# A whole decoder trunk ordered by the scheduler's other model machine

## The chip, the cores and the metric

One Trainium2 chip, one of its cores. The metric is the device time of one execution in microseconds (us): the median of several runs of the kernel before is 1920.45 us (three runs, 1916.95 to 1922.32). The engines are TensorE (PE, with its weight loads PEld), VectorE (DVE), ScalarE (ACT), GpSimd (POOL) and the queues of SyncE (SP), which issues most DMAs. Each engine works through its own list of instructions in order; semaphores hold an instruction until what it reads is there.

## What is computed

A trunk of two layers on 512 tokens of width 1024 in float32. A layer is a feed-forward part, a mix of tokens, and another feed-forward part, each behind a norm and with shift, scale and gate from a condition vector:

```python
def swiglu(x, w_in, w_out):
    gate, up = jnp.split(x @ w_in, 2, axis=-1)
    return (jax.nn.silu(gate) * up) @ w_out
```

RWKV's step over the tokens, per head:

```python
def step(S, inp):
    r_t, w_t, k_t, v_t, kk_t, a_t = inp
    s_kk = jnp.einsum('bhvk,bhk->bhv', S, kk_t)
    S = (S * w_t[:, :, None, :] - s_kk[..., None] * (kk_t * a_t)[:, :, None, :]
         + v_t[..., None] * k_t[:, :, None, :])
    return S, jnp.einsum('bhvk,bhk->bhv', S, r_t)
```

The mix projects the normed tokens to three groups side by side, and projects their joined outputs back: attention over a window of 128 keys with sinks (8 query heads, 2 key heads), four RWKV heads of width 64, and a gated convolution over three tokens.

## The kernel before

**Products.** Activations lie with the features on the partitions. A float32 product is made of three products of two-part numbers: ACT casts the high part (`wH`, L101), DVE subtracts it from the source to make the low part (`wL`, L102), and PE adds high x high, high x low and low x high in one bank (`mm3`, L90 to L92; `mm6`, L98, over two halves of 256 tokens). Weights come over SP's queue (`load_w`, L267), and each block of 1024 columns costs one cast on ACT and one subtraction on DVE. The feed-forward parts make their products in pairs with fewer multiplications (L441 to L443). What this text calls a product is one matmul of 256 columns.

**Norm.** The sum of squares goes over the partitions on PE (`ps_ss`, L229); ACT and DVE make the reciprocal root (`rstd`, L231 and L232); PE spreads it (`ps_rstd`, L239); DVE multiplies (`hn_t`, L249), ACT and DVE write the two parts `hnH` and `hnL` (L250, L256), which the next part's first products read. It is done for two halves of the tokens. `close` writes the order of DVE and ACT there by hand; PE's order is left to the scheduler.

**Mix.** Four pieces are written as generators and laid side by side by a program of credits (`RWKV_WORK`, `ATT_WORK`, `FILL_WORK`): the products of the projections (`ps_mm`), attention in four blocks of 128 tokens, and RWKV in two halves `q` of two heads each, whose tiles carry the digit 0 or 1 at the end of their names. A block of attention makes scores (`ps_sc`), a softmax on DVE and ACT (`mx`, `es`, `den`, and `Sc` normalised at L1062), a transpose (`ps_pt`, L1069) and the weighted sum (`ps_av`). A half of RWKV works on chunks of 64 tokens: reciprocals of decays (`iP`, L791) and norms (`rn`, L792), pair products (`ps_c` to `B` and `K`), the inverse of a triangular matrix: 16 x 16 blocks by elimination on DVE (`elim`, `inv`, L855 and L856, with round trips through DRAM over SP's queue before and behind), and from the block diagonal `T` (L915) two levels of products of four quadrants (`quads`: `ps_T`, `ps_x`, `ps_t`, `ps_tt`, `ps_w2`). Then come `ps_gn` (to `GT` and `N`), `ps_o`, six steps over the chunks (`ps_s` on PE, `St` on DVE, L989 and L990), `ps_ys`, and the group norm: `gnsq`, `ps_v`, `gnrs` with a reciprocal of 512 columns (L1004), L1005, L1006, the gate `ps_g` and L1013. Its result is split to `yrH` and `yrL`, the last inputs of the mix's output products, whose last two tiles (`ps_mm` 7300 and 7362 in the first layer) finish the token halves one after the other.

**What sets the order.** The program is written in one order; a scheduler then puts each engine's instructions in another, by a model machine that gives each instruction a duration and a priority by its place in the text. Where the kernel has `tc.manual_schedule`, the written order of the named engines is kept inside that stretch. Tiles in pools and their buffer numbers are dealt out as before.

Of the kernel before, what the change touches and what calls it, by code (L numbers as in the profile page):

```python
# [56 lines left out]
@with_exitstack  # L57
def trunk_kernel(ctx, tc, ins, out, layers=L, phases=("ffn1", "mix", "ffn2")):
    nc = tc.nc
    PSUM = bass.MemoryType.PSUM  # L60
    const = ctx.enter_context(tc.tile_pool(name="const", bufs=1))
    small_ = ctx.enter_context(tc.tile_pool(name="small", bufs=2))
# [5 lines left out]
    sp = ctx.enter_context(tc.tile_pool(name="sp", bufs=2))  # L68
    ps = ctx.enter_context(tc.tile_pool(name="ps", bufs=4, space=PSUM))
    dram = ctx.enter_context(tc.tile_pool(name="dram", bufs=1, space=bass.MemoryType.DRAM))  # L70
# [1313 lines left out]
```

## Time and profile before

| | |
|---|---|
| median of three runs | 1920.45 us |
| the profiled execution | 1921.27 us |
| its span from the first to the last instruction | 1919.3 us |
| mean granted TensorE clock | 0.992 |
| DMA, mean over the span | 161 GB/s |
| feed-forward parts and mixes, roughly | mixes from 398.6 to 624.5 and from 1340 to 1569 us, the rest feed-forward |

The profile is of one execution, and times below are microseconds from the start of its span. Its busy times are shares of that span; the clock is the share of full speed that the throttle granted. A view of stretches gives, for each stretch, the busy time of PE, PEld, DVE, ACT and POOL with the number of instructions in brackets. A timeline's row has the start, the duration, the engine, the line, the output and the inputs, and in square brackets how long the engine had been idle before and who released it.

### The profile page before, as it was taken

The page shows a single profiled execution, that of the slowest core. Times are in us where ns is not written, and L with a number is a line of the kernel's source. Part 1 is how long each engine was busy: PE and PEld are TensorE (multiplying, and loading weights), DVE is VectorE, ACT ScalarE, POOL GpSimd, SP SyncE. Part 2 cuts the span into 40 slices and gives each one's busy share as a digit, 9 for nine tenths or more (in the row PEclk, how much of TensorE's full clock was granted, in tenths as well). Part 3 has the DMA queues.
Part 4 walks back from the last instruction along what each step waited for, and adds up shares of the span by engine and source line. Part 5 has one row for each costly group of instructions (what it writes and reads, how often), then busy time and mean ns, then how long its engine had stood idle before and what let it go on. Part 6 is the DMA issues. An engine that isn't in the chain of part 4 may idle for free. (4 is left out here: it accounts for less than half of the span.)

```text
span 1919.3 us, 37594 instructions
## 1 busy us (share of the span) xinstructions
PE 1876.9 (98%) x15744; PEld 1737.6 (91%) x15744; DVE 1395.9 (73%) x2185; ACT 847.0 (44%) x1292; POOL 130.7 (7%) x212
## 2 busy tenths in 40 slices
PE   8999999999999999999999999999998999999999
PEld 7998899987789999899899988989877899988998
DVE  7687687758966877677877776876598668873862
ACT  4443355356432554155345514544563335532551
POOL 0101101000000001110100020010000000110000
PEclk8999999999999999999999999999999999999999
DMA  7767877421312476887726687781211215764741
GB/s 299 252 163 228 261 195 241 153 69 47 86 39 75 124 196 181 272 218 200 259 79 179 169 272 227 197 276 44 89 55 49 87 34 156 213 213 134 197 139 59
DMA packets 104457, 308.50 MB, mean 161 GB/s; under 512 B 23520, under 2 KB 24544, under 8 KB 103264
## 3 DMA queue, kind: packets, MB, share of 16 engines
q1 hardware_dynamic: 76064, 203.33, 32.3%
q0 software_dynamic: 28224, 102.77, 21.5%
q8 instruction: 123, 2.02, 0.4%
q14 instruction: 46, 0.38, 0.1%
HBM read 302.66 MB, written 3.41 MB: 159 GB/s over the span
## 5 line engine op out<-in xcount | busy, mean ns | idle before, releaser
L101 ACT CAST wH<-wraw 128x1024 fp32r<-128x1024 f32 (+2 forms) x292 | 268.2, 922 | 512.0 <-PE ps_mm L91 162.0
L102 DVE TENSOR_TENSOR wL<-wraw,wH 128x1024 fp32r<-128x1024 f32 (+2 forms) x292 | 308.3, 1059 | 97.1 <-ACT wH L101 96.3
L90 PE MATMUL ps_mm<-actH,wH 128*128 128x512 f32 (+1 forms) x784 | 288.5, 368 | 0.0
L91 PE MATMUL ps_mm<-actL,wH 128*128 128x512 f32 (+1 forms) x784 | 288.0, 367 | 0.0
L92 PE MATMUL ps_mm<-actH,wL 128*128 128x512 f32 (+1 forms) x784 | 288.0, 367 | 0.0
L441 PE MATMUL ps_d<-comH,wH 128*128 128x256 f32 x816 | 226.7, 278 | 1.4 <-ACT wH L101 0.8
L443 PE MATMUL ps_d<-comH,wL 128*128 128x256 f32 x816 | 225.7, 277 | 2.3 <-DVE wL L102 2.3
L442 PE MATMUL ps_d<-comL,wH 128*128 128x256 f32 x816 | 225.4, 276 | 0.0
L98 PE MATMUL ps_mm<-hnH,wH 128*128 128x256 f32 x1040 | 215.9, 288 | 5.0 <-ACT hnH L101 2.9
L98 PE MATMUL ps_mm<-hnL,wH 128*128 128x256 f32 x1040 | 213.9, 284 | 0.0
L98 PE MATMUL ps_mm<-hnH,wL 128*128 128x256 f32 x1040 | 209.1, 282 | 0.5 <-DVE wL L102 0.5
L163 DVE SCALAR_TENSOR_TENSOR wada<-wada,crep 128x1024 f32<-128x1024 f32 x140 | 168.1, 1220 | 55.9 <-DMA wada<-in_wadaT 55.7
L102 DVE TENSOR_TENSOR wL<-sum,wH 128x1024 fp32r<-128x1024 f32 x102 | 124.9, 1224 | 73.7 <-ACT wH L101 73.6
L98 PEld LDWEIGHTS ps_mm<-hnH,wH 128*128 128x128 f32 x1040 | 160.8, 191 | 16.3 <-issue 7.9
L92 PEld LDWEIGHTS ps_mm<-actH,wL 128*128 128x128 f32 x784 | 147.8, 189 | 24.3
L91 PEld LDWEIGHTS ps_mm<-actL,wH 128*128 128x128 f32 x784 | 147.8, 189 | 24.2
L90 PEld LDWEIGHTS ps_mm<-actH,wH 128*128 128x128 f32 x784 | 147.8, 189 | 24.2
L98 PEld LDWEIGHTS ps_mm<-hnL,wH 128*128 128x128 f32 x1040 | 161.4, 191 | 7.1 <-issue 6.2
L101 ACT CAST wH<-sum 128x1024 fp32r<-128x1024 f32 x102 | 107.5, 1054 | 136.5 <-PE ps_d L442 60.1
L98 PEld LDWEIGHTS ps_mm<-hnH,wL 128*128 128x128 f32 x1040 | 160.2, 191 | 4.7 <-issue 3.4
L441 PEld LDWEIGHTS ps_d<-comH,wH 128*128 128x128 f32 x816 | 153.3, 188 | 3.5 <-ACT wH L101 1.4
L443 PEld LDWEIGHTS ps_d<-comH,wL 128*128 128x128 f32 x816 | 153.2, 188 | 2.9 <-DVE wL L102 2.9
(404 smaller groups left out, 4238.1 us busy)
## 6 DMA issues: line engine op xcount, KB each, us to landing
wada<-in_wadaT POOLq DMA_DIRECT2D x128, 512.0 KB, 4.9
wraw<-in_wmi SPq DMA_DIRECT2D x40, 512.0 KB
wraw<-in_w2p SPq DMA_DIRECT2D x36, 512.0 KB
wraw<-in_w1p SPq DMA_DIRECT2D x32, 512.0 KB
wraw<-in_w1o SPq DMA_DIRECT2D x32, 384.0 KB
wraw<-in_w2o SPq DMA_DIRECT2D x32, 384.0 KB
wraw<-in_w1i SPq DMA_DIRECT2D x20, 512.0 KB
wraw<-in_w1o SPq DMA_DIRECT2D x32, 320.0 KB
```

Source lines behind the costliest of these rows:

```text
L90: mm(acc, wH, xH, start=start, stop=False)
L91: mm(acc, wH, xL, start=False, stop=False)
L92: mm(acc, wL, xH, start=False, stop=stop)
L98: mm(acc[:, sl], w[a][:, k], x[b][:, sl], start=start and n == 0 and sl is HALVES[0], stop=stop and n == 2, skip_group_check=True)
L101: nc.scalar.copy(hi, src)
L102: nc.vector.tensor_sub(lo, src, hi.bitcast(F32))
L163: stt(w, w, 1.0, crep, ALU.mult, ALU.mult, accum_out=out_)
L441: mm(pt[:, i], wH, x[k][0], start=start and i + k == 0, stop=False, skip_group_check=True)
L442: mm(pt[:, i], wH, x[k][1], start=False, stop=False, skip_group_check=True)
L443: last = mm(pt[:, i], wL, x[k][0], start=False, stop=k == 3, skip_group_check=True)
```

## The change

One line opens a block of the scheduler around the whole program, with another model machine. Before, the program stood in the block that is open at the start and was ordered by the default one. No instruction is written differently; the lines behind move by one, and so do the numbers of tiles.

```diff
 @with_exitstack
 def trunk_kernel(ctx, tc, ins, out, layers=L, phases=("ffn1", "mix", "ffn2")):
     nc = tc.nc
+    ctx.enter_context(tc.block(schedule_with_timeline_sim=True))
     PSUM = bass.MemoryType.PSUM
```

PE has 14292 matmuls and POOL the same list in both. ACT gets four activation-table loads more (22 for 18), two in each mix, since its activations alternate in another way. Three places show the new order.

The first is PE at the end of RWKV's second half in the first layer, the kernel before: `ps_ys` is the last product with the state, `ps_v` the sum of the group norm; `y0` to `y5` are outputs of attention and convolution, which are long done.

```order
L995 MATMUL ps_ys_7022<-RT1_6813,St1_6811 64x64 x14
L98 MATMUL ps_mm_7015<-y5H_6608,wH_7010 128x256 x2
L98 MATMUL ps_mm_7015<-y5L_6609,wH_7010 128x256 x2
L98 MATMUL ps_mm_7015<-y5H_6608,wL_7011 128x256 x2
L98 MATMUL ps_mm_7015<-y0H_6598,wH_7010 128x256 x2
```

The same place with the change: `yrH_7132` and `yrL_7133` are the parts of the first half's output, `yrH_7136` is the second half's.

```order
L990 MATMUL ps_s_6973<-St1_6812,GT1_6709 64x64 x2
L990 MATMUL ps_s_6983<-St1_6812,GT1_6709 64x64 x2
L990 MATMUL ps_s_6999<-St1_6812,GT1_6709 64x64 x2
L996 MATMUL ps_ys_7023<-RT1_6814,St1_6812 64x64 x14
L612 MATMUL ps_v_7059<-gnsq_7057,con_85 128x512
L1013 MATMUL ps_g_7099<-gd_5856,gw_5988 128x512
L99 MATMUL ps_mm_7180<-yrH_7132,wH_7160 128x256 x2
L99 MATMUL ps_mm_7180<-yrL_7133,wH_7160 128x256 x2
L99 MATMUL ps_mm_7180<-yrH_7132,wL_7161 128x256 x2
L99 MATMUL ps_mm_7225<-yrH_7132,wH_7220 128x256 x2
L99 MATMUL ps_mm_7225<-yrL_7133,wH_7220 128x256 x2
L99 MATMUL ps_mm_7225<-yrH_7132,wL_7221 128x256 x2
```

What moved: the products that stood between the last steps, `ps_ys`, `ps_v` and `ps_g` are ahead of them, as are those of the tiles 7084 and 7091 that read only `y0` to `y5`; 12 products are left ahead of the first that reads `yrH_7136`.

The second is PE at the norm behind the first layer's mix, with the change; `hnH` is what the next feed-forward part reads.

```order
L91 MATMUL ps_mm_7363<-yrH_7136,wH_7086 128x256
L92 MATMUL ps_mm_7363<-yrL_7137,wH_7086 128x256
L93 MATMUL ps_mm_7363<-yrH_7136,wL_7087 128x256
L230 MATMUL ps_ss_7317<-ones_r_110,ss_4117 128x1
L230 MATMUL ps_ss_7317<-ones_r_110,sq_7290 128x1
L230 MATMUL ps_ss_7317<-ones_r_110,sq_7299 128x1
L230 MATMUL ps_ss_7317<-ones_r_110,ss_4117 128x1
L230 MATMUL ps_ss_7317<-ones_r_110,sq_7290 128x1
L230 MATMUL ps_ss_7317<-ones_r_110,sq_7299 128x1
L240 MATMUL ps_rstd_7336<-con_85,rstd_7324 128x128 x2
L230 MATMUL ps_ss_7399<-ones_r_110,ss_4117 128x1
L91 MATMUL ps_mm_7476<-hnH_7140,wH_7214 128x256
```

What moved: before, the 24 products of the tile 7362 (7363 here) stood between `ps_rstd` and that `ps_ss`, and nine of the tile 7300 around the first `ps_ss`; all of them are ahead of it now.

The third is DVE in the middle of the first mix, the kernel before, where attention's second block normalises its scores (`Sc_4577`) and RWKV's second half has not begun:

```order
L635 SCALAR_TENSOR_TENSOR r0_4988<-ps_mm_4939,par_102,r0_4988 128x511
L1060 TENSOR_TENSOR den_4613<-den_4613,es_4610 128x4
L1061 RECIPROCAL den_4613<-den_4613 128x4
L1062 TENSOR_TENSOR Sc_4577<-Sc_4577,den_4613 128x512
L1073 TENSOR_TENSOR pmc_4642<-ps_pt_4637,con_84 128x512
```

The same rows with the change:

```order
L1061 TENSOR_TENSOR den_4614<-den_4614,es_4611 128x4
L784 SCALAR_TENSOR_TENSOR P1_5935<-decay_5888,zero_112 128x64
L829 TENSOR_TENSOR B0_5116<-ps_c_5117,con_85 128x512
L1062 RECIPROCAL den_4614<-den_4614 128x4
L786 COPY pc1_5944<-P1_5935 128x8
L792 RECIPROCAL iP1_5949<-P1_5935 128x512
L829 TENSOR_TENSOR B0_5116<-ps_c_5118,con_85 128x512
L811 TENSOR_TENSOR AR1_6005<-r1_5691,P1_5935 128x512
L1063 TENSOR_TENSOR Sc_4578<-Sc_4578,den_4614 128x512
```

What moved: rows of both RWKV halves, the reciprocal `iP1` among them, stand between the softmax's sum and the normalising that `ps_pt` waits for.

## The prediction

> **What bounds the kernel now.** I read the page's busy shares first, then TensorE's waits, then the stretches of one mix.
>
> ```profile
> PE 1876.9 (98%) x15744; PEld 1737.6 (91%) x15744; DVE 1395.9 (73%) x2185; ACT 847.0 (44%) x1292; POOL 130.7 (7%) x212
> ```
>
> PE is the bound: 42.4 us of the 1919.3 us span are idle on it. No instruction leaves the program, so a new order can gain only PE's idle time and what PE loses at half clock. The waits view names where the idle time is:
>
> ```profile
> engine line waited for: us in total, times, longest us
> PE ps_o L976 <- DVE St L969: 5.1, 2, 2.6
> PE ps_mm L98 <- ACT hnH L101: 2.9, 1, 2.9
> ```
>
> The first stands in the mixes, once in each layer; the second is the program's start. The stretches of the first mix, from its first head sum (`ps_ks`, 398.6) to the norm sum of the next sub-layer (`ps_ss`, 624.5), and the middle of the second mix:
>
> ```profile
> 398.60:440.00 41.40, 40.89 (x321) 35.88 (x322) 21.16 (x35) 22.50 (x46) 0.00 (x0) 1.00 0.32 95
> 440.00:476.00 36.00, 34.53 (x273) 27.61 (x271) 32.92 (x76) 24.38 (x62) 0.42 (x2) 1.00 0.12 39
> 476.00:523.00 47.00, 45.35 (x443) 37.37 (x441) 44.04 (x104) 19.64 (x45) 0.43 (x2) 1.00 0.26 73
> 523.00:548.00 25.00, 20.98 (x563) 18.43 (x563) 15.78 (x55) 6.27 (x17) 0.00 (x0) 0.93 0.20 42
> 548.00:604.00 56.00, 53.79 (x803) 48.18 (x802) 35.03 (x57) 17.47 (x29) 0.00 (x0) 0.97 0.27 84
> 604.00:624.50 20.50, 20.50 (x163) 19.36 (x162) 15.69 (x20) 7.16 (x12) 0.00 (x0) 1.00 0.08 27
> 1465.00:1490.00 25.00, 21.15 (x552) 18.29 (x543) 15.06 (x53) 7.01 (x18) 0.00 (x0) 0.93 0.18 35
> ```
>
> Columns: stretch, its length, busy time of PE, PEld, DVE, ACT and POOL, granted clock, DMA. Three things are to be seen. PE's idle time in the six stretches is 0.5 + 1.5 + 1.7 + 4.0 + 2.2 + 0.0 = 9.9 us, and the clock below 1 costs 0.07 x 25 + 0.03 x 56 = 3.4 us more: **13.3 us per mix is all that a better order can win back** there, most of it in 523 to 604, where the inverse's chain has too few products between its steps. DVE is busy for 77.0 of the 83 us from 440 to 523: in the middle it is about as full as PE. And the last stretch, 604 to 624.5, has no idle time at all: its long chain is wholly covered today.
>
> **The change part by part.** DVE, ACT, PE and SP get another order; the kinds and sizes stay. In the feed-forward parts the pieces of order show swaps among neighbours with the same products ahead of the same weights; I cost them at nothing, since PE there waits for weight conversions (DVE's L102 before all) whose own order stays; were that cover gone, a swap would cost one conversion, 1.2 us. ACT's four added table loads hide behind PE work in the same way. What the change does move is the mix. The new order sends the projection products out early, as filling between the steps of attention and of both RWKV halves (between the first half's `ps_T` and its `ps_gn` stand 103 products where 20 stood). That filling is what 523 to 604 lacks. But the products are the same ones, so they are missing behind it:
>
> *The tail of the second half.* Now 18 products stand between `ps_ys` and `ps_v`, 18 between `ps_v` and `ps_g`, and behind `ps_g` 30 more of `ps_mm` 7084 and 7091 that need no `yr`, besides those that need the first half's alone. In the new order nothing stands between `ps_ys`, `ps_v` and `ps_g`, and 12 products behind them; the next reads `yrH` of the second half, which ends this chain:
>
> ```profile
> 602.49 0.57 PE L995 MATMUL ps_ys<-RT,St 64*64 64x64 f32 x14
> 603.11 0.62 DVE L996 TENSOR_TENSOR y<-y,ps_ys 128x448 f32<-128x448 f32 x1
> 603.85 0.63 ACT L1000 ACTIVATE gnsq<-y 128x512 f32<-128x512 f32 x1 [1.77 <-DVE y L996]
> 605.16 1.02 PE L611 MATMUL ps_v<-gnsq,con 128*128 128x512 f32 x2
> 606.22 0.69 ACT L1003 ACTIVATE gnrs<-ps_v,v_gneps 128x512 f32<-128x512 f32 x1 [1.74 <-PE ps_v L611]
> 606.94 3.35 DVE L1004 RECIPROCAL gnrs<-gnrs 128x512 f32<-128x512 f32 x1 [3.21 <-ACT gnrs L1003]
> 610.78 0.74 DVE L1005 SCALAR_TENSOR_TENSOR y<-y,par,gnrs 128x512 f32<-128x512 f32 x1
> 612.58 0.74 DVE L1006 SCALAR_TENSOR_TENSOR y<-y,par,bonus 128x512 f32<-128x512 f32 x1
> 613.42 0.69 DVE L1013 TENSOR_TENSOR y<-y,ps_g 128x512 f32<-128x512 f32 x1
> 614.15 0.62 ACT L101 CAST yrH<-y 128x512 fp32r<-128x512 f32 x1 [5.73 <-DVE y L1013]
> ```
>
> The durations behind `ps_ys` sum to 0.62 + 0.63 + 1.02 + 0.69 + 3.35 + 0.74 + 0.74 + 0.69 + 0.62 = 9.1 us, with the hand-overs that the rows show (0.04 to 0.12 each, DVE's own overlapping) 9.25. Beside it PE has `ps_v` (1.0), `ps_g` (about 0.5) and 12 products at about 0.115 (1.4): **6.4 us idle** where none is now. Half clock followed the shorter idle time of 2.55 us:
>
> ```profile
> 541.24 0.34 PE L976 MATMUL ps_o<-B,AX 64*64 64x64 f32 x8 [2.55 <-DVE St L969]
> ```
>
> The stretch around it lost 0.07 x 25 = 1.75 us to the clock; I add **1.7**. In a sentence apart: the Trainium skill ("TensorE: Matmul & The Clock Gate", Part 1: The HAM clock gate) has the array at half clock after an idle window of about 3.4 us and back after a busy one of that length; by it the 6.4 us here bring one such window and the 2.7 us below none, where the trace, which throttled after 2.55 us, would allow another 1.7 us per mix there. The trace so far speaks for the shorter bound; the sum goes without that second window.
>
> *The norm behind the mix.* Now 24 products of `ps_mm` 7362 stand between `ps_rstd` and the first product that reads `hnH`, and 9 of `ps_mm` 7300 among the `ps_ss` rows; all 33 go ahead of `ps_ss`. The chain:
>
> ```profile
> 625.68 0.58 PE L229 MATMUL ps_ss<-ones_r,sq 128*128 128x1 f32 x4
> 626.37 0.26 ACT L231 ACTIVATE rstd<-ps_ss,v_eps 128x2 f32<-128x2 f32 x1 [1.56 <-PE ps_ss L229]
> 626.93 0.66 PE L239 MATMUL ps_rstd<-con,rstd 128*128 128x128 f32 x4
> 627.60 1.23 DVE L102 TENSOR_TENSOR wL<-wraw,wH 128x1024 fp32r<-128x1024 f32 x1 [0.77 <-ACT wH L101]
> 628.74 0.87 DVE L249 SCALAR_TENSOR_TENSOR hn_t<-h,gmod,ps_rstd 128x256 f32<-128x256 f32 x2
> 629.31 0.91 ACT L250 ACTIVATE hnH<-hn_t,mod 128x256 fp32r<-128x256 f32 x2 [1.75 <-DVE hn_t L249]
> ```
>
> DVE and ACT keep this order, the conversion ahead of `hn_t` too. From the end of `ps_ss` (626.26) to the first of the two `hnH` (629.31 + about 0.5) it is 3.5 us; PE has `ps_rstd` (0.66) and one `ps_ss` (0.14) in it: **2.7 idle**. The 33 products themselves are paid in either order.
>
> *Three steps without filling.* The last three `ps_s` of the second half stand back to back before `ps_ys`, where 8 to 12 products stood between:
>
> ```profile
> 545.33 0.33 PE L989 MATMUL ps_s<-St,GT 64*64 64x64 f32 x4
> 546.26 0.33 PE L989 MATMUL ps_s<-St,GT 64*64 64x64 f32 x4
> ```
>
> A step takes 0.93 us from one to the next, 0.33 of it on PE: 3 x 0.6 = **1.8**.
>
> *Waits behind DVE's reciprocals.* The new DVE order puts long reciprocals ahead of short rows that PE waits for: `iP` of the second half ahead of the normalising of `Sc` of attention's second block, which `ps_pt` reads, and `gnrs` of the first half ahead of `GT`, `N` and `St` of the second, which `ps_o` reads. DVE is in order, so PE's queue behind `ps_pt` and `ps_o` waits too. The trace has no such wait; it has the reciprocal (3.35, above). Bounds: nothing, if PE reaches the waiter later than DVE does, which the trace of a DVE 77/83 busy speaks against; and 5 x 3.35 = 16.8 if each of the mix's reciprocals but the tail's stood before a waiter. I take the two that the order shows, **6.7**.
>
> *What is won.* I take all of the **13.3** as gained. Sum per mix: 6.4 + 1.7 + 2.7 + 1.8 + 6.7 - 13.3 = +6.0; the second mix shows the same idle time (3.9 us in its row against 4.0), so two mixes make +12.0.
>
> *Outside the mixes.* At the close of the first feed-forward part the products between `ps_rstd` and the first `hnH` product go too:
>
> ```profile
> 374.32 0.60 PE L239 MATMUL ps_rstd<-con,rstd 128*128 128x128 f32 x4
> 376.29 0.91 ACT L250 ACTIVATE hnH<-hn_t,mod 128x256 fp32r<-128x256 f32 x2 [1.68 <-DVE hn_t L249]
> ```
>
> 20 products now precede `ps_rstd` and cover its inputs; behind it `hn_t` and `hnH`, about 0.5 each, stay bare: +1.0. At the start more warm products and earlier weight conversions stand before the first product:
>
> ```profile
> 21.32 0.80 PE L98 MATMUL ps_mm<-hnH,wH 128*128 128x256 f32 x2 [2.86 <-ACT hnH L101]
> ```
>
> Of the 2.9 us I take 1.5 as gained (0 to 2.9); a swap at the second projector gains 0.5. Together -1.0.
>
> Sum: +12.0 - 1.0 = +11.0. The profiled execution took 1921.27 us (1.97 around its span), 0.82 above the median: 1932.3 there, **1931.5** against the median of 1920.45.
>
> **The rivals.** *The chain really comes earlier: 1911.* The mark is `T` of the second half.
>
> ```profile
> 457.01 3.35 DVE L791 RECIPROCAL iP<-P 128x512 f32<-128x512 f32 x1
> 547.94 0.69 DVE L915 TENSOR_TENSOR T<-C,con 128x512 f32<-128x512 f32 x1
> 457.00:548.00 91.00, 84.35 (x1162) 70.97 (x1160) 78.82 (x195) 39.81 (x94) 0.85 (x4) 0.98 0.19 49
> ```
>
> From `iP` to `T` pass 90.9 us, 78.8 of them DVE work. The new order puts 7.3 us more DVE work between the two rows (12.5 of attention and convolution in, 5.2 out, from their traced durations), but lets `iP` start 6.9 us earlier, since attention's second block stands behind it. If DVE's 12 idle us shrink to 4 or 5, `T` comes 7.3 us earlier, with 5.8 us less product work left behind it and the 3.9 us of idle time and clock after 548 gone: -7.3 - 5.8 - 3.9 + 12.6 (the bare chains, without the reciprocals' waits) = -4.4 per mix, with the -1.0 -9.8 in all. Against it: attention's rows now alternate with DVE's long ones.
>
> *Balance: 1918.* Bare chains 12.6, no wait behind reciprocals, all 13.3 won: -0.7 per mix, -2.4 in all. It decides for this if PE reaches `ps_pt` and `ps_o` after DVE's reciprocal.
>
> *Every reciprocal counts: 1952.* 16.8 in place of 6.7 makes +16.1 per mix, +31.1 in all. The point from which it decides: DVE with no idle time from `iP` on.
>
> *Nothing happens: 1920.* The order of every engine but POOL differs, so this is nearly excluded.
>
> **How the numbers follow.** Forecast 0.50, earlier chain 0.17, balance 0.20, every reciprocal 0.10, nothing 0.03. About 0.3% (5.8 us) is what a measurement can tell from no change. Faster: most of the earlier chain and a quarter of the balance, 0.19; slower: the forecast less 0.03 and the worst case, 0.57; within: 0.24. The range from 1905 to 1949 takes in the earlier chain with 6 us of error and stops short of the worst case. The slower cases alone reach from 1926 to 1955.
>
> **What would show it.** Right: PE idle 6 to 7 us between `ps_g` and the first product of the second half's `yr`, with half clock behind; 2.5 to 3 us ahead of the first `hnH` product after each mix; `ps_pt` waiting for DVE's `Sc`, `ps_o` for `St` of the second half; no wait of 2.6 us at the first half's `ps_o`. Wrong: a `ps_ss` after the mix less than 222 us behind `ps_ks` (225.9 now), or a feed-forward part that changes by over 2 us, which I costed at nothing.

## The result and the profile after

| | before | after |
|---|---|---|
| median of four runs | 1919.54 us | 1943.74 us (1941.03 to 1947.21) |
| after / before, 95% interval | | 1.0127 [1.0104, 1.0150] |
| span of the profiled execution | 1919.3 us | 1942.7 us |
| mean granted TensorE clock | 0.992 | 0.985 |

The changed kernel is slower by 24.2 us; the forecast was 11. The page of the changed kernel, busy times:

```profile
PE 1878.6 (97%) x15744; PEld 1743.8 (90%) x15744; DVE 1388.3 (71%) x2185; ACT 851.6 (44%) x1296; POOL 130.8 (7%) x212
```

PE does the same work (1.7 us more busy time) and is idle for 64.1 us of its span where it was idle for 42.4. The waits of PE in the changed kernel (what waits, for whom; us in total, times, the longest):

```profile
PE ps_mm L99 <- DVE y L1014: 9.2, 2, 4.8
PE ps_s L990 <- DVE St L991: 6.7, 7, 3.3
PE ps_mm L91 <- ACT hnH L251: 5.2, 3, 2.1
PE ps_sc L1035 <- DVE Sc L1042: 4.9, 2, 2.7
PE ps_v L612 <- ACT gnsq L1001: 4.2, 4, 1.5
PE ps_T L885 <- DVE T L916: 2.9, 2, 2.3
PE ps_pt L1070 <- DVE Sc L1063: 2.9, 4, 0.9
```

The largest wait of before, 2.6 us at the first half's `ps_o` in each mix, is gone. In its place stand the tail (first row, twice 4.4 to 4.8), the norm (third row), and waits inside the chains of the mix.

Where the time went is read from stretches between marks that both kernels have: the first mix's `ps_ks`, the first `hnH` product behind each mix, the one behind the second feed-forward part, and the second mix's `ps_ks`. Columns: stretch, length, busy time of PE, PEld, DVE, ACT and POOL, granted clock, DMA share, GB/s. Before, then after:

```profile
0.00:398.55 398.55, 390.05 (x2840) 367.77 (x2840) 297.76 (x451) 174.70 (x237) 38.92 (x68) 0.98 0.68 216
398.55:630.42 231.87, 222.00 (x2608) 192.80 (x2609) 167.42 (x349) 99.89 (x211) 0.85 (x4) 0.99 0.22 65
630.42:974.28 343.86, 341.66 (x2522) 322.58 (x2520) 264.59 (x367) 158.60 (x213) 34.69 (x54) 1.00 0.69 202
974.28:1339.89 365.61, 360.90 (x2674) 340.94 (x2673) 275.16 (x393) 166.45 (x228) 35.66 (x56) 1.00 0.64 188
1339.89:1574.97 235.08, 222.97 (x2608) 193.53 (x2609) 167.42 (x349) 99.89 (x211) 0.85 (x4) 0.98 0.22 64
1574.97:1919.30 344.33, 339.31 (x2501) 320.03 (x2499) 223.53 (x281) 147.43 (x194) 19.75 (x26) 1.00 0.56 156
```

```profile
0.00:397.75 397.75, 390.23 (x2840) 368.83 (x2840) 295.92 (x451) 176.34 (x237) 38.95 (x68) 0.98 0.68 217
397.75:639.23 241.48, 219.50 (x2609) 192.41 (x2609) 167.28 (x348) 101.23 (x213) 0.86 (x4) 0.97 0.22 62
639.23:985.88 346.65, 344.65 (x2517) 325.80 (x2517) 260.75 (x362) 157.04 (x211) 34.70 (x54) 0.99 0.68 201
985.88:1355.00 369.12, 363.02 (x2677) 342.69 (x2675) 275.41 (x399) 167.98 (x232) 35.67 (x56) 1.00 0.64 186
1355.00:1595.29 240.29, 219.26 (x2608) 191.40 (x2609) 167.29 (x348) 101.36 (x213) 0.86 (x4) 0.97 0.22 63
1595.29:1942.70 347.41, 341.95 (x2498) 322.68 (x2498) 221.68 (x282) 147.62 (x195) 19.77 (x26) 0.99 0.55 155
```

Row by row the change is -0.8, +9.6, +2.8, +3.5, +5.2 and +3.1 us, +23.4 in all. In the mixes it is idle time: 241.48 - 219.50 = 22.0 us idle in the first where 9.9 were, and 21.0 where 12.1 were in the second, while PE's busy time fell by 2.5 and 3.7. In the feed-forward stretches behind the mixes it is not idle time (2.0 against 2.2, 5.5 against 5.0) but busy time, +3.0 and +2.6, at a clock of 0.99: half clock at their beginning, as the last view of this section shows for the first.

The tail of the second half, PE's timeline after the change (start, duration, and in brackets the idle time before and its releaser):

```profile
610.84 2.07 PE L612 MATMUL ps_v<-gnsq,con 128*128 128x512 f32 x2 [1.52 <-ACT gnsq L1001]
612.70 1.68 PE L1013 MATMUL ps_g<-gd,gw 128*128 128x512 f32 x2
613.69 0.93 PE L99 MATMUL ps_mm<-yrH,wH 128*128 128x256 f32 x2
...
619.44 0.79 PE L99 MATMUL ps_mm<-yrH,wH 128*128 128x256 f32 x2 [4.36 <-DVE y L1014]
```

The 12 products behind `ps_g` are all there is, and PE then stands 4.36 us for the chain through DVE's reciprocal. The norm behind it:

```profile
636.30 0.71 PE L240 MATMUL ps_rstd<-con,rstd 128*128 128x128 f32 x4 [0.55 <-DVE rstd L233]
...
639.23 1.01 PE L91 MATMUL ps_mm<-hnH,wH 128*128 128x256 f32 x3 [2.10 <-ACT hnH L251]
```

Idle 0.55 + 2.10 = 2.65 us. The clock around tail and norm, in the view of stretches:

```profile
610.60:625.00 14.40, 9.80 (x39) 7.68 (x40) 7.12 (x7) 1.59 (x4) 0.00 (x0) 0.64 0.00 1
637.90:645.00 7.10, 5.77 (x28) 5.77 (x29) 5.63 (x14) 3.60 (x8) 0.00 (x0) 0.52 0.23 74
```

### The profile page after: what moved, and what is told of

Same layout as the page of the kernel before. It is cut to its first block, busy times and chain, and to the rows that moved or that the text cites. A ratio compares the mean times of both kernels' runs of the same rounds, so it can differ in the third digit from the quotient of the medians.

```text
span 1942.7 us, 37597 instructions
## 1 busy us (share of the span) xinstructions
PE 1878.6 (97%) x15744; PEld 1743.8 (90%) x15744; DVE 1388.3 (71%) x2185; ACT 851.6 (44%) x1296; POOL 130.8 (7%) x212
## 4 chain that ended last, share of the span: by engine, by line
PE 78%; DVE 12%; DMA 4%; issue 2%; ACT 2%; SPq 1%; POOL 0%; DVEq 0%; ACTq 0%; POOLq 0%
PE ps_mm L99 14%; PE ps_mm L91 9%; PE ps_mm L92 9%; PE ps_mm L93 9%; PE ps_d L444 6%; PE ps_d L442 6%; PE ps_d L443 6%; PE ps_f L442 3%; PE ps_f L444 3%; PE ps_f L443 3%; DVE wL L103 2%; PE ps_g L444 2%; PE ps_g L443 1%; PE ps_g L442 1%; ACT wH L102 1%
```

## The experiments

Ratios are to the kernel before, measured on the same chip, with 95% intervals. An expectation that says "faster than after" compares with 1.0127.

**1. The norm's order, given back and taken away.** In `norm_written` the changed kernel keeps the written order of PE in `close`:

```diff
-    HAND = {mybir.EngineType.DVE, mybir.EngineType.Activation}
+    HAND = {mybir.EngineType.DVE, mybir.EngineType.Activation, mybir.EngineType.PE}
```

> The changed kernel, with the order of PE in the closes kept as written, so that the products that stood around ps_ss and behind ps_rstd stand there again; the tails of the mixes stay as changed. Theory A (the bare norm costs its idle time and the half clock behind it): per mix 2.1 us ahead of the first hnH product, 0.55 ahead of ps_rstd, 2.9 behind it at half clock, 11 in two mixes, 1.2 at the first close and 2.6 at the second layer's projector: 15 us less than the changed kernel, about 1929 us. Theory B (the idle time alone counts, the clock comes back by itself at no cost): 7 us less, about 1937.

1937.12 us, 1.0090 [1.0067, 1.0112]: 7 us won (give or take 6), the size of theory B. The run does not decide between the theories, though, since it doesn't simply take the bare norm away: the waits for `hnH` behind the mixes go, but with fewer products ahead of `ps_ss` PE now waits 1.8 us there in the first mix and 1.5 in the second, and the first has 6.8 us of half clock behind that wait. The sum of squares `ss` comes late on DVE, which works off five rows of `h` (3.1 us) ahead of it; the 33 products that the model machine puts ahead had covered that. In `before_norm_bare` the kernel before gets the bare norm of the changed one, in the mixes alone:

```diff
-            run(pt, seq, hi_, True, ((4, lambda: stats(lo_, sqs)), (7, lambda: spread(lo_))))
+            run(pt, seq, hi_, True)
+            run(pt2, seq2, hi_, True)
+            stats(lo_, sqs)
+            spread(lo_)
```

> The kernel before, with nothing changed but PE's order in the close of the mixes: all products of the last two tiles ahead of ps_ss, ps_rstd and the hnH products bare behind it. Theory A (idle time and half clock): 2 x 5.5 = 11 us more than the kernel before, about 1931. Theory B (idle time alone): 2 x 2.7 = 5.4 more, about 1925. If the norm was not the place, no change: 1920.

1930.60, 1.0056 [1.0039, 1.0074]: 10.4 us for two bare norms, as theory A said. The waits alone are 0.6 + 1.6 and 0.6 + 2.1 us, 4.9 in all; half clock for 6.8 us follows each norm in that profile.

**2. The tail.** `tail_behind` issues the products of the last two tiles that need no `yr` behind `ps_v`; `norm_tail` is this and `norm_written` together.

```diff
...
+                    with tc.issue_after(got["pv"]):
                         mm3(pt[:, : T // 2], w, k, xs[k], HALVES[0], n == 0, False)
```

> The changed kernel, with the 36 products of the last two output tiles that read only y0 to y5 queued behind ps_v of the second half in both mixes; norms stay bare. Theory A (the tail's cover was taken away and nothing needed it where it went): 4.4 to 4.8 us of idle time ahead of the first yr product and about 2.4 at half clock behind it go, in two mixes 14 us less than the changed kernel, about 1930. Theory B (the filling is only moved: what the tail wins the state's steps lose, which had these products between them): 0 to 5 us less, 1939 to 1944.

> Both edits together. If the two costs add (theory A of both): 29 us less than the changed kernel, about 1915, faster than the kernel before by about 5. If the half clock is shared between the tail and the norm behind it: 22 to 25 less, about 1920. Theory B of both: about 10 less, 1934.

`tail_behind`: 1934.35, 1.0077 [1.0061, 1.0094], 9 us won, between the two theories (14, and 0 to 5). `norm_tail`: 1933.10, 1.0070 [1.0050, 1.0090], 11 us won, as theory B of both said. By the medians the two gains do not add up (7 and 9 give 11), but the shortfall of 5 to 6 us is no larger than its error, some 8 us from these intervals. The tail's wait for `y` is gone in both, but other waits grow: in `tail_behind` those of the steps `ps_s` rise from 6.7 to 10.0 us, and in `norm_tail`, where they are 4.5, 4.9 us come at `ps_tt`. The wait at `ps_ss` stands in `norm_tail` too, 1.8 us in the first mix, so the late tail is not what makes the sum of squares late. That these waits are the products now missing there is a reading, not shown.

**3. The clock by itself.** Idle products (float32, 128 x 128, into a bank that nobody reads) fill a wait without ending it earlier. `after_warm` puts twenty into the tail and ten into the norm of each mix.

```diff
...
+            if tiles[0][1] is not None:
+                warm_by(last_r[0], 10, "r0")
...
+            if q:
+                warm_by(sq, 20, R)
```

> The changed kernel with idle products in its two longest bare stretches of each mix: twenty behind ps_g of the second group (the tail's wait for yr) and ten behind ps_rstd (the norm's wait for hnH). Its order is otherwise that of after, but for some forty places on PE at the second mix. Waits stay as long as they are, since nothing that is waited for comes earlier. After has half clock for 6.8 us behind the tail and 6.8 us behind the norm in each mix: four stretches, 13.6 us lost. Theory A (half of what the change costs is half clock behind bare stretches): 10 to 13 us less than after, 1931 to 1934. Theory B (the waits make the price): within 2 us of after.

1934.61, 1.0081 [1.0063, 1.0100], 9 us won (give or take 6), a little under theory A's 10 to 13. Not all of it need be the idle products': in the profiled execution the second mix is 4.6 us ahead of after's already at the first half's `ps_gn`, before any idle product of that mix, and from there PE's order differs in some forty places. From the second half's `ps_v` on, where the idle products work, that profile is 2.7 us shorter behind the first mix and 4.2 behind the second, most of it (2.1 and 2.4) in the feed-forward stretch behind the norm. The stretch behind the first norm ran at full clock in this kernel (the last but two column), where it was 0.52:

```profile
639.00:646.00 7.00, 6.51 (x55) 6.41 (x56) 5.78 (x13) 4.09 (x9) 0.00 (x0) 1.00 0.25 75
```

From the first `hnH` product to the one behind the second feed-forward part it takes 344.52 us, against 346.65 in after and 343.86 in before. The same on the other side: `bare_warm` is `before_norm_bare` with ten idle products behind `ps_rstd`, and `before_warm` the kernel before with five behind a wait of 1.1 us at the second half's `ps_s`.

> The run before_norm_bare (before with the mixes' norm bare, 1930.6) with ten idle products of 0.18 us behind the ps_rstd spread, in the wait for hnH; nothing else moves. That run's profile has half clock for 6.8 us behind each of the two norms. Theory A (half clock is the larger part of what a bare norm costs): the two stretches go, 2 x 3.4 = 6.8 us less than before_norm_bare, near 1924, and what is left over before (3 to 4 us) is the wait itself, some 2 us for each mix. Theory B (the wait alone makes the price): 1930, no change.

> The kernel before with five idle products (fp32, 128x128, into a PSUM tile that nobody reads) put behind the first ps_s step of the second RWKV group in each mix; no other instruction moves on any engine. In the profile of before this stretch (589 to 592) has a wait of 1.11 us and is followed by half clock: 3.4 us at 592.8 in the first mix, 6.8 us at 1534.8 in the second, which costs (3.4 + 6.8) / 2 = 5.1 us. Five products of about 0.18 us fit into the wait. Theory A (a short bare stretch costs its wait and then half of the half-clock stretch behind it): both stretches go and the time is 5 us less than before, near 1915. Theory B (only the waits count, and the half clock costs nothing or comes anyway): within 1 us of before, or up to 2 us more where the idle products are in the way.

`bare_warm`: 1927.49, 1.0044 [1.0028, 1.0059], 2 us less than before_norm_bare by the ratios, which is within their error, and not 7. The idle products fell into half clock themselves and came 1.6 us too long:

```profile
632.73 0.71 PE L245 MATMUL ps_rstd<-con,rstd 128*128 128x128 f32 x4 [0.61 <-DVE rstd L238]
633.27 4.03 PE L86 MATMUL ps_idle<-con,rstd 128*128 128x128 f32 x20
637.14 0.28 PE L235 MATMUL ps_ss<-ones_r,ss 128*128 128x1 f32 x2
```

So this run doesn't price the clock. `before_warm`: 1918.69, 1.0000 [0.9990, 1.0009], theory B. Of the half clock that was to go, one stretch of 3.4 us went and one of 6.8 became 3.4, and nothing was won: in that profile PE waits 1.8 and 2.5 us at the `ps_s` just ahead of the idle products, where before waits 0.45 and 1.8. I read the runs so: half clock costs time where a queue of ready products follows, as behind the norm, and little where PE soon waits for a chain again; the second half of this is argued, not shown.

**4. One wait inside the mix.** In after two `wL` conversions that wait for a DMA stand ahead of the second `St` on DVE, and PE's `ps_s` stands 3.31 us (ACT's `wH`, DVE's `wL` and `St`):

```profile
569.02 1.78 ACT L102 CAST wH<-wraw 128x1024 fp32r<-128x1024 f32 x2 [4.21 <-DMA wraw<-in_wmo]
570.10 2.09 DVE L103 TENSOR_TENSOR wL<-wraw,wH 128x1024 fp32r<-128x1024 f32 x2 [3.05 <-ACT wH L102]
572.11 0.28 DVE L991 SCALAR_TENSOR_TENSOR St<-ps_s,pc,N 128x64 f32<-128x64 f32 x1
```

`after_st` issues DVE's `wL` of the last three `wo1` tiles behind the first half's last `St` (the edge binds DVE alone, not ACT's `wH` as the expectation has it):

```diff
...
+        with tc.issue_after(late.ins) if late else nullcontext():
+            split(wH[:, :n], wL[:, :n], w[:, :n])
```

> The changed kernel with the conversions of the last three wo1 tiles (ACT wH, DVE wL) issued only behind the first group's last St step, as they stand in before; in after two of them stand ahead of the second St on DVE and wait for a DMA, and PE stands 3.31 us at the second ps_s of the first mix, with half clock for 3.4 us behind it; in the second mix the same place costs 0.58 and 1.27 us. Theory A (this wait is on the path to the end): 3.3 + 1.7 + about 1 = 4 to 6 us less than after, near 1939. Theory B (the second group's chain sets the end of the mix whatever the first does, and the tail's wait grows by what is won here): within 1.5 us of after.

1942.64, 1.0131 [1.0112, 1.0150]: nothing won, theory B. The 3.31 us are gone, and other waits took their place: `ps_v` rises from 4.2 to 5.7 us, a wait of 2.1 us comes at the second half's `ps_o` of the first mix, and the tail there stands 4.8 us where it stood 4.36.

**5. Products held back in the front.** If the model machine's early products were the cause, holding them behind the first half's `ps_gn` should help. `hold18` holds the last two input projections and the first six `wo1` tiles, `hold19` leaves one projection free.

```diff
+                with hold(n):
                     mm6(pt, w, k, hn[k], k == 0, k == KD - 1)
...
+                    with tc.issue_after(got["gn"].ins):
                         mm6(pt, w, k, xs[k], k == 4, k == 3)
```

> The changed kernel with the products of the last two input projections (tiles 18 and 19 of 20) and of the first six wo1 tiles issued only behind the first RWKV group's last ps_gn product; the model machine then orders everything else anew. In after these products run ahead of the first group's chain: its ps_o comes at 560.6 (541.2 in before), and by the tail of the second group no products are left. Theory A (products put ahead of the chains are what the change costs; the end of the mix is then a bare chain): ps_o of the first group comes back by 8 to 15 us, the second group's tail finds products to run and its wait of 4.4 to 4.8 us goes, and the time is 6 to 14 us less than after, 1930 to 1938, although the held stretch itself is left without filling. Theory B (the chain is held up by DVE and ACT, products only fill its waits): ps_o comes at about the same time, the held stretch stands bare, and the time is 0 to 10 us more than after.

> As hold18, but only the last input projection (tile 19) and the six wo1 tiles are held behind the first group's ps_gn; tile 18 (48 products, 5.6 us) stays free to fill the chain's waits. Theory A: between after and hold18 in where ps_o comes, with less bare time in the held stretch: 6 to 12 us less than after. Theory B: 0 to 6 us more than after.

1956.00, 1.0201 [1.0184, 1.0218], and 1945.90, 1.0145 [1.0132, 1.0158]. My theory A fell, and `hold18` cost 14 us more than after where theory B had at most 10. The first half's `ps_o` came 5.5 and 3.1 us earlier, not 8 to 15; the held front stood bare (PE's waits at `ps_T` rise from 2.9 us to 9.9 in both); and the tail stood as in the changed kernel, in both runs:

```profile
PE ps_mm L99 <- DVE y L1016: 9.6, 2, 4.8
```

**6. Engines and halves of the mix in the order of before.** Every instruction of the two mixes on the named engines is tied to its predecessor in the order of before, and the model machine orders the rest.

```diff
...
+    for row in rows_of_before:
+        for x, y in zip(row, row[1:]):
+            tc.add_manual_dep(traced[y], x, nosync)
```

> The changed kernel with PE, DVE and ACT tied to the order of before in the two mixes, norms included; the start, the feed-forward layers and the second projector stay as the model machine orders them. By the marks of the two profiles the mixes with the stretches behind them hold 14.8 + 6.1 of the 23 us, and the second projector 3: before plus 1 to 4 us, 1920 to 1924. Were the loss spread over the program (a rival), it would stay above 1930.

> The changed kernel, with DVE's 1528 instructions of the two mixes tied to the order that they have in before (an issue-order edge from each to the next); PE, ACT and SP are ordered by the model machine around that. Theory C (the cause lies in DVE's order: in after it prepares the second RWKV group 27 us earlier, attention ends 47 us later, at 548, and both groups' chains then queue on DVE): most of the mixes' loss goes, 12 to 18 us less than after, 1926 to 1932. Theory D (the cause lies in PE's order: the model machine takes every product as soon as it can run, so that none is left beside the last chain): the tail stays bare, 0 to 6 us less than after.

> The changed kernel with PE's instructions of the two mixes (3884 by their numbers) tied to the order of before, and the other engines ordered by the model machine around that. Theory D: most of the mixes' loss goes, 12 to 18 us less than after. Theory C: PE now waits in the order of before for results that DVE still makes in the model machine's order; between 6 us less and 10 us more than after.

> The changed kernel with ACT's instructions of the two mixes tied to the order of before. ACT is busy 44% of the span and no long wait of PE in after names it as the first cause, so both theories expect within 4 us of after.

| tied | us | ratio |
|---|---|---|
| PE, DVE, ACT (`mix_kept`) | 1925.42 | 1.0033 [1.0021, 1.0046] |
| DVE alone | 2028.58 | 1.0573 [1.0553, 1.0592] |
| PE alone | 1980.59 | 1.0319 [1.0299, 1.0338] |
| ACT alone | 2025.77 | 1.0553 [1.0532, 1.0574] |

(DVE's tied instructions are 764 in both mixes together, not 1528.) The order of the mixes, with their norms and the half clock behind them, holds 1.0127 - 1.0033, some 18 of the 24 us (give or take 5); 1.0033 is 6.4 us, where I had expected 1 to 4. All three expectations for a single engine fell: one engine in the old order among others in the new is far worse than either order, with PE waiting 15 to 21 us ahead of `ps_pt` alone. These orders fit together or don't; a mixture has costs of its own, which must be kept in mind for the halves too. Then by halves: `front_kept` ties all three engines up to the second half's `ps_o`, `back_kept` from the second half's first `St` to the end of the norm.

> As mix_kept, but PE, DVE and ACT are tied to the order of before only in the front of each mix, up to the second group's ps_o; from there (the last chain's ps_s steps, the tail, the norm) the model machine orders. Theory E (the loss lies in the tail and the norm, the other order of the front is mostly slack): the tail's wait of 4.8 us, the norm's 0.55 + 2.10 us and the half clock behind both stand as in after, and the time is mix_kept plus 2 x 7.5 to 2 x 10 us, 1938 to 1945. Theory F (the front's order makes both chains late, tail and norm only show it): the tail's wait shrinks below 2 us, and the time is 1926 to 1934.

> The opposite: only the back of each mix (from the second group's first St to the norm's end) is tied to the order of before on PE, DVE and ACT; the front is ordered by the model machine, which lets the first group's last ps_s steps stand without products there. Theory E: no wait at the tail nor at the norm, and mix_kept plus 2 to 8 us, 1926 to 1934. Theory F: the front's lateness appears as waits at the second group's ps_gn, ps_o or ps_s, and the time stays within 6 us of after, 1938 to 1946.

1943.22, 1.0139 [1.0121, 1.0156], and 1940.43, 1.0119 [1.0103, 1.0135]: theory E was right on the first, theory F on the second, and with either half in the order of before nearly the whole loss stays. The waits of `front_kept`, then of `back_kept`:

```profile
PE ps_mm L99 <- DVE y L1014: 9.6, 2, 4.8
PE ps_o L977 <- DVE St L970: 6.1, 3, 2.5
PE ps_mm L91 <- ACT hnH L251: 5.2, 3, 2.1
```

```profile
PE ps_s L990 <- ACT y L985: 15.8, 2, 8.1
PE ps_o L977 <- DVE N L967: 7.9, 2, 4.0
```

With the front of before, tail and norm stand bare as in after: so the back of the new order is enough for them. With the back of before, they don't, but PE waits ahead of the second half's `ps_o` and its first `ps_s`. The larger wait, 8.1 and 7.8 us at `ps_s`, was 0.4 and 1.8 us in before. The tie keeps ACT's conversions of output weights ahead of `y`, as in before; the first half's `y` is late here, and with it `yrH` and the conversion that stands behind it on ACT and DVE. Only when that one ends, at 587.7, does SP issue the next loads of output weights (576.9 in before), and the conversions that stand ahead of `y` wait for them:

```profile
591.32 1.78 ACT L102 CAST wH<-wraw 128x1024 fp32r<-128x1024 f32 x2 [4.65 <-DMA wraw<-in_wmo]
597.11 1.04 ACT L102 CAST wH<-wraw 128x1024 fp32r<-128x1024 f32 x1 [4.01 <-DMA wraw<-in_wmo]
599.78 0.70 ACT L985 COPY y<-ps_o 128x256 f32<-128x256 f32 x2 [1.63 <-DVE RT L984]
```

So the 15.8 us at `ps_s` come from joining a late front to the old back, and this run doesn't show that the new front by itself costs nearly the whole loss. The wait of 4.0 us is the reciprocal that the prediction named, here in `back_kept`:

```profile
578.50 3.35 DVE L1005 RECIPROCAL gnrs<-gnrs 128x512 f32<-128x512 f32 x1 [2.74 <-ACT gnrs L1004]
581.77 0.36 DVE L966 TENSOR_TENSOR GT<-ps_gn,con 128x256 f32<-128x256 f32 x1
```

**7. A version that beats both.** The largest wait of before is `ps_o` of the first half: `ps_gn` ends at 537.0, but DVE finishes the other half's elimination before it turns to `GT`, `N` and `St`. `before_gt` puts the last seven elimination steps behind that `St`.

```diff
+                hold = tc.issue_after(got["first"].ins) if q and s == 8 else nullcontext()
...
+                with hold:
+                    tt(t, G[:, s, s + 1 :].unsqueeze(2).to_broadcast([NT, n, s + 1]), ...)
```

> The kernel before, with the second half of the second group's elimination (steps 8 to 14, on DVE) issued behind the first group's GT, N and first St, which wait there for nothing but their turn on DVE: in before ps_gn ends at 537.0, GT starts at 539.7 when the elimination is through, and PE stands 2.55 us at ps_o, with half clock for 3.4 us behind it, in both mixes. Theory A (this wait is on the path to the end): ps_o starts 2.5 us earlier, the half clock there goes, and the time is 2 x (2.55 + 1.7) = 8.5 us less than before at most, 1910 to 1915. Theory B (the second group's chain sets the end; it is put off here by the 1.65 us of the four operations and the copy that now stand ahead of the elimination's rest): within 2 us of before, or up to 3 us more.

1911.34 against 1917.78, 0.9968 [0.9954, 0.9981]: 6.2 us won (3.6 to 8.8), theory A with three quarters of its size. DVE and PE there:

```profile
540.30 0.18 DVE L971 COPY St<-N 128x64 f32<-128x64 f32 x1
540.40 0.21 DVE L857 TENSOR_TENSOR elim<-G,inv 64x63 f32<-64x63 f32 x1
...
540.59 0.34 PE L980 MATMUL ps_o<-B,AX 64*64 64x64 f32 x8
```

`ps_o` starts without a wait, the clock of the stretch is 1.00 in both mixes, and a wait of 1.2 us for `y` comes at the first `ps_s`.

## Why the prediction was right in sign and half in size

By its own terms, against the marks of the two profiles:

| term | forecast | measured |
|---|---|---|
| both mixes with their norms | +12.0 | +14.8 |
| feed-forward behind a mix | 0 | +5.9 |
| second projector | -0.5 | +3.5 |
| start and first close | -0.5 | -0.8 |
| sum | +11.0 | +23.4 |

The steps that failed are, by these marks: the half clock behind the norm, put at nothing (+5.9); the second projector, put at a gain (4.0 off); and, inside the mixes, the gain of 13.3, which did not come as a whole, and the reciprocals' 6.7, a wait that isn't there. That the mixes' sum is only 2.8 off is luck: these two errors have opposite signs. Without the 6.7 the forecast for a mix would have been -0.7, so the right sign, too, hung on that wait.

**The tail** was right: 6.4 us idle forecast, 1.52 ahead of `ps_v` + 4.36 ahead of `yrH` = 5.9 measured, and 1.52 + 4.80 = 6.3 in the second mix. Its half clock, 1.7 forecast, lasted 6.8 us in each mix (from 617.4 and 1573.2), of which 4.8 and 4.2 fell on products behind the wait: 2.4 and 2.1 lost, by the granted 0.50. **The bare norm**, 2.7 forecast, is 2.65. The **steps without filling** cost less, two waits of 0.39 in each mix where I had 1.8.

**The second clock window failed: it was left out of the sum, and its size was wrong.** I named 1.7 us per mix of half clock behind the norm and put nothing into the sum. It came, in both mixes, for 6.8 us and not 3.4, and fell on dense products: +3.0 and +2.6 of busy time in the stretches behind, which I had costed at nothing. It is also what I had named as a sign of being wrong, a feed-forward part that changes by over 2 us. `before_norm_bare` has a price of the same kind on the other kernel (10.4 us for two norms, of which 4.9 are waits), and `after_warm`, which ends no wait earlier, has these stretches 2.1 and 2.4 us shorter than after. In a sentence apart: by the idle window of about 3.4 us that the Trainium skill ("TensorE: Matmul & The Clock Gate", Part 1: The HAM clock gate) gives, the 2.65 us bring no half clock; the trace has 6.8 us of it behind them, so here the measurement decides.

**Waits behind reciprocals, 6.7 per mix, were taken for the wrong thing.** `ps_pt` waits for `Sc` 2.9 us in the whole program, at most 0.9 at a time, and `ps_o` of the second half does not wait for `St` or `N`. The reciprocal `gnrs` does stand ahead of `GT` in after:

```profile
586.31 3.35 DVE L1005 RECIPROCAL gnrs<-gnrs 128x512 f32<-128x512 f32 x1 [2.78 <-ACT gnrs L1004]
589.58 0.36 DVE L966 TENSOR_TENSOR GT<-ps_gn,con 128x256 f32<-128x256 f32 x1
```

It costs PE no wait there: 48 products stand ahead of `ps_o` in PE's order and run without a gap to 592.5, and the last `N` is ready at 590.9. It is those products, not the reciprocal, that `ps_o` comes behind. Its room in the sum was taken by waits I had not foreseen: `ps_sc` (4.9), `ps_T` (2.9) and `St` behind a conversion that waits for a DMA (3.3).

**The gain of 13.3 per mix failed as a term of its own.** I booked all idle time of before as won and the bare chains as lost, as if they were separate. The wait at the first `ps_o` did go, but PE's idle time rose from 9.9 to 22.0 us in the first mix and from 12.1 to 21.0 in the second. The traces show where the chains become late. The first half's block diagonal `T` and its first `ps_gn`, before and then after:

```profile
522.44 0.67 DVE L915 TENSOR_TENSOR T<-C,con 128x512 f32<-128x512 f32 x1
535.33 0.34 PE L958 MATMUL ps_gn<-beN,AX 64*64 64x64 f32 x8
```

```profile
520.58 0.69 DVE L916 TENSOR_TENSOR T<-C,con 128x512 f32<-128x512 f32 x1 [0.84 <-DMA C<-di]
557.07 0.34 PE L959 MATMUL ps_gn<-beN,AX 64*64 64x64 f32 x8
```

`T` is 1.9 us earlier in after and `ps_gn` 21.7 us later: 36.5 us pass between them where 12.9 did. PE starts 109 products there where it started 20, and rows of attention (`ps_sc`, `ps_pt`, `ps_av`), of which before has none. The second half's `T` is 5.0 us earlier (542.94 against 547.94), and its `ps_o` 10.0 later (592.47 against 582.5). The prediction had counted these products, 103 in place of 20, but as filling that wins idle time back; since PE works through its list in order, they also stand in the chain's way. The 89 more, at about 0.115 us, make some 10 us, an estimate from these rows; what makes the rest isn't shown. So the rival of the earlier chain had its mark right, an earlier `T`, and its consequence wrong. (The `iP` at 457.01 that it starts from is the first half's; the second half's own starts at 500.33.)

That the products of a mix are one stock, so that a wait filled in one place comes back in another, is how I read these runs, and it isn't shown. That holding the early products back undoes the loss is excluded by `hold18` and `hold19`, which leave the front bare in exchange; that restoring one engine's order undoes it, by the three runs with one engine tied. Neither excludes the early products, or one engine's order, as where the loss begins.

**The second projector failed in sign.** A swap was to win 0.5; the new order reads `hnL` too early, three times (0.27, 0.67 and 1.07), and waits once for a weight's `wH` (0.57) and once for `silu` (1.17):

```profile
1001.75 0.38 PE L92 MATMUL ps_mm<-hnL,wH 128*128 128x256 f32 x1 [0.67 <-DVE hnL L257]
...
1005.13 0.39 PE L92 MATMUL ps_mm<-hnL,wH 128*128 128x256 f32 x1 [1.07 <-DVE hnL L257]
...
1009.60 0.51 PE L99 MATMUL ps_mm<-hnH,wH 128*128 128x256 f32 x2 [1.17 <-ACT silu L531]
```

Together these are 3.75 us, and 3.4 us at half clock follow; before had 0.9 us of idle time there. No other loss is seen in the feed-forward products, which were costed at nothing.

What stays open: which of the rows between `T` and `ps_gn`, products, attention or the other half's, makes the chains late (`hold18`, which holds eight tiles' products back, still has `ps_gn` at 550.6); what each half of the new order costs apart from the joint; and 3 to 4 us of `mix_kept`'s 6.4, which its profiled execution (span 1920.5) doesn't show.

## What to carry to other kernels

When a new order moves filling work, don't add up "waits filled" and "waits laid bare" as separate terms: count how much filling is left at the last chain, look whether the filling that moved now stands ahead of a chain's own rows, and expect a wait taken out in one place to come back in another unless the chain itself gets shorter. Price a bare stretch by its idle time and by the half clock behind it, the second above all where a full queue of products follows. What won here was not a new order of everything but five short operations put ahead of another chain's long run on the engine that PE was waiting for.

## What the runs showed of the hardware

Half clock came in every run in stretches of 3.4 us or multiples (6.8, 10.2, 13.7, 17.1), and it doesn't take a long idle time: in `bare_warm` it followed 3.4 us in which PE was busy for 2.8, with twelve rows of `ps_ss` of one column and a single wait of 0.61 us. The view of stretches, before and in the half clock (the last but two column):

```profile
630.00:633.40 3.40, 2.79 (x26) 2.71 (x25) 0.17 (x1) 1.19 (x2) 0.00 (x0) 1.00 0.02 5
633.40:636.80 3.40, 3.40 (x19) 3.40 (x18) 2.89 (x5) 1.11 (x4) 0.00 (x0) 0.50 0.31 92
```

The twenty rows of idle products that began at 633.27 took 4.03 us, where the same twenty took 2.40 in `after_warm`.
